# Rotary in two steps, its scratch in the normed input's room, and the filter weights off GpSimd

## The chip, the cores and the metric

The kernel runs on one core of a Trainium2 chip. The metric is the device time of one execution, in microseconds (us). The kernel before took 1338.2 us, the median of 3 runs (1337.94 to 1339.54).

## The reference

A two-layer encoder on 512 tokens of width 1024, all in float32. Only three places matter here:

```
layer 0: mixed = [gated_deltanet, dilated_attention](rmsnorm(x) @ ab_w_in) @ ab_w_out
layer 1: mixed = [retention, hyena](rmsnorm(x) @ cd_w_in) @ cd_w_out
each layer: x = x + mixed;  x = x + conv_ffn(rmsnorm(x))

rope(t):  t1, t2 = halves of each head's 64 columns
          [t1*cos - t2*sin, t1*sin + t2*cos]          # q and k of dilated attention and retention
hyena_filters:  hid = sin(f1*(z @ w1 + b1));  hid = sin(f2*(hid @ w2 + b2))
                filt = (hid @ w3) * exp(-t*deltas)     # a forward and a backward filter
```

## The kernel before

**Tiling.** Activations stand transposed, features on the 128 partitions and the 512 tokens along a row. A float32 product is made of three matmuls of float32r parts (`mm3`, lines 266 to 268): high times high, high times low, low times high. So each weight tile `raw` that a DMA brings is split into `whi` by ScalarE (line 254) and `wlo` by VectorE, or GpSimd when `pool_lo` is set (line 255). `raw` has 3 buffers; `whi` and `wlo` have 4 each, so the cast of a tile waits for the projection four tiles earlier.

**Rotary.** The projections q0, k0, q1, k1 of dilated attention (q0, q1, k0, k1 of retention) leave 128x512 tiles in PSUM (`first0` to `first2`, and `dqk` or `rqk` for the fourth). For each in turn `rope_stack` has ScalarE copy the tile to `rt` (line 455, 2 buffers; from now on "the reading"), four DMAs on SyncE's queue swap halves into `rs` (line 458, 1 buffer), GpSimd multiplies `rs` by the sines (line 459), VectorE multiplies `rt` by the cosines and adds (lines 460, 461), and ScalarE, VectorE and, for the moving operand, GpSimd write the high and low parts (lines 466 to 470). The four PSUM buffers tagged `acc` then take the four accumulators `pt0` to `pt3` of the token-major value projection (`proj_tok`, line 295), whose four weight tiles each hold 6 matmuls for each accumulator: 96 in all.

**Filters.** `hyena_filters` is a generator that `hyena` steps once after each of its twelve column projections (`hap`), apart from the numbers in `HSKIP`, counted from 0. The first step makes the first sine layer (matmul `hm`, line 1098, chain `san` on VectorE, sine `mlp` on ScalarE, line 1078). The second prepares the parts of the last weight `w3` (sum and difference `ws` on GpSimd, `wy` on ScalarE and GpSimd, `wl` on VectorE, zeroed by GpSimd) and makes the second sine layer (matmul `hm`, line 1111, up to `hx`). The third and later ones multiply (`fp`, lines 1131 and 1132) and transform. Between them `turn` transposes the product `u` (line 1209) on TensorE (`tp`, line 1195).

**Order.** Except at the start, a scheduler turns the program into one fixed order for each engine; an instruction that waits holds up all behind it on its engine. The normed input's tiles `xn` (pool `xp`, 2 buffers of 4 KB a partition) are free once TensorE has transposed them.

Of the kernel before, what the change touches and what calls it, by code (L numbers as in the profile page):

```python
# [8 lines left out]
F32 = mybir.dt.float32  # L9
F32R = mybir.dt.float32r  # L10
# [5 lines left out]
S = 512  # L16
# [147 lines left out]
class K:  # L164
# [282 lines left out]
        self.nc.sync.dma_start(rope, self.I["rope"])  # L447
        return rope

    def rope_stack(self, pool, rope, ps, moving, tag, bufs, scale=1.0):  # L450


        nc = self.nc
        t = pool.tile([128, S], F32, tag="rt", name="rt", bufs=2)
        nc.scalar.mul(t, ps, scale)  # L455
        sw = pool.tile([128, S], F32, tag="rs", name="rs", bufs=1)
        for q in range(4):
            nc.sync.dma_start(sw[32 * q:32 * q + 32, :], t[32 * (q ^ 1):32 * (q ^ 1) + 32, :])
        nc.gpsimd.tensor_mul(sw, sw, rope[:, 1, :])
        nc.vector.tensor_mul(t, t, rope[:, 0, :])  # L460
        nc.vector.tensor_add(t, t, sw)
        o = pool.tile([128, 4 if moving else 2, S], F32R, tag=tag, name=tag, bufs=bufs)
        half = [slice(0, 64), slice(64, 128)]
        for e in range(2):
            a, b = half[e], half[1 - e]
            nc.scalar.copy(o[a, e], t[a])
            nc.vector.tensor_sub(o[a, 2 + e] if moving else o[b, e], t[a], o[a, e])
            if moving:
                nc.gpsimd.memset(o[b, 2 + e].bitcast(F32), 0.0)
                nc.gpsimd.tensor_copy(o[b, e], o[a, e])  # L470
        return o

    def mm_stack(self, out, a, b, e, cols):
        self.nc.tensor.matmul(out, a[:, e, cols], b[:, e], start=True, stop=False)
        self.nc.tensor.matmul(out, a[:, e, cols], b[:, 2 + e], start=False, stop=True)
# [14 lines left out]
    def dilated(self, n, tail):  # L490
        nc, I = self.nc, self.I
        V = nc.vector
        with ExitStack() as ctx:
            dp = ctx.enter_context(self.tc.tile_pool(name="dil", bufs=1))
            rope = dp.tile([128, 2, S], F32, name="rope")
            lnc = dp.tile([128, 896], F32, name="lnc")
            v = dp.tile([128, NT, 512], F32, name="dv")
            qk, sm, pT, op = {}, {}, {}, {}
            yh, yl = self.y_tiles()

            def project(p, what, ps=None):
                if ps is None:
                    ps = self.acc(nm="dqk")
                    self.proj_t(self.get(), n, ps)
                qk[p, what] = self.rope_stack(dp, rope, ps, what == "k", "d" + what, 3)

            def scores(p, i):
                st = self.sm.tile([128, 6], F32, tag="st", name="st", bufs=8)
                o = 384 - 128 * i
                for e in range(2):  # L510
                    sp = self.wk(nm="sp")
                    self.mm_stack(sp, qk[p, "q"], qk[p, "k"], e, slice(i * 128, i * 128 + 128))
                    s_ = dp.tile([128, S], F32, tag="smx", name="smx", bufs=6)
                    V.tensor_tensor_reduce(s_, sp, lnc[:, o:o + 512], scale=-0.125, scalar=3e38, op0=ALU.add, op1=ALU.min, accum_out=st[:, e:e + 1])
                    nc.scalar.activation(s_, s_, AF.Exp, scale=-1.0, bias=st[:, e:e + 1], accum_out=st[:, 2 + e:3 + e])
                    sm[p, i, e] = s_
                V.reciprocal(st[:, 4:6], st[:, 2:4])
                for e in range(2):
                    nc.gpsimd.tensor_scalar(sm[p, i, e], sm[p, i, e], st[:, 4 + e:5 + e], 1.0, op0=ALU.mult, op1=ALU.mult)

            def turn(p, i):
                for e in range(2):
                    tp = TPD(self)((128, 4, 128), "tp")
                    for j in range(4):
                        nc.tensor.transpose(tp[:, j, :], sm[p, i, e][:, j * 128:j * 128 + 128], self.ident)
                    t = dp.tile([128, 4, 128], F32, tag="pT", name="pT", bufs=4)
                    (V.tensor_copy if e else nc.scalar.copy)(t, tp)
                    pT[p, i, e] = t

            def pv(p, i):  # L530
                if i == 0:
                    op[p] = self.acc(nm="op")
                for j in range(4):
                    for e in range(2):
                        h = 2 * p + e
                        nc.tensor.matmul(op[p][64 * e:64 * e + 64, i * 128:i * 128 + 128], v[:, j, h * 64:h * 64 + 64], pT[p, i, e][:, j, :], start=(j == 0), stop=(j == 3))
                if i == 3:
                    self.split(yh[p // 2][:, p % 2, :], yl[p // 2][:, p % 2, :], op[p])

            ps = self.first(n, range(4), at=DAT)  # L540
            self.pool_lo = False
            nc.sync.dma_start(rope, I["rope"])
            nc.sync.dma_start(lnc, I["lnc"])
            for i in range(4):
                project(i // 2, "qk"[i % 2], ps[i] if i < 3 else None)
            self.proj_tok(n, lambda t, a: nc.scalar.copy(v[:, t, :], a))
            later = [(2, "q"), (2, "k"), (3, "q"), (3, "k")]
            units = [(p, i) for p in range(4) for i in range(4)]
            for u in range(len(units) + 3):
                if u < len(units):  # L550
                    scores(*units[u])
                if 0 <= u - 2 < len(units):
                    turn(*units[u - 2])
                if 0 <= u - 3:
                    pv(*units[u - 3])
                if later and u in DPROJ[:4]:
                    project(*later.pop(0))
                if u in DPROJ[4:]:
                    next(tail, None)
            return self.by_tile(self.y_list(yh, yl))  # L560
# [430 lines left out]
    def retention(self, n, order):  # L991
        nc, I = self.nc, self.I
        V = nc.vector
        with ExitStack() as ctx:
            rp = ctx.enter_context(self.tc.tile_pool(name="ret", bufs=1))
            rope = self.load_rope(rp)
            gen = rp.tile([128, 4, 896], F32, name="gen")
            ps = self.first(n, order)
            qk = {}
            for i in range(4):  # L1000
                which, s = i // 2, i % 2
                if i < 3:
                    pp = ps[i]
                else:
                    pp = self.acc(nm="rqk")
                    self.proj_t(self.get(), n, pp)
                qk[which, s] = self.rope_stack(rp, rope, pp, which == 0, f"r{which}{s}", 1, 1.0 if which else 0.125)
            v = rp.tile([128, NT, 512], F32, name="rv")
            Z = rp.tile([128, NT, 512], F32, name="rz")
            self.proj_tok(n, lambda t, a: nc.scalar.copy(v[:, t, :], a))  # L1010
# [48 lines left out]
    @staticmethod  # L1059
    def g4(hp, nm, dt=F32):  # L1060
        return hp.tile([128, 2, S], dt, tag="g4", name=nm, bufs=G4)
# [18 lines left out]
    def hyena_filters(self, hp, H):  # L1080


        nc, I = self.nc, self.I
        V = nc.vector
        g4 = lambda nm, dt=F32: self.g4(hp, nm, dt)
# [9 lines left out]
        w3 = g4("w3")[:64]  # L1095
        nc.sync.dma_start(w3, I["hy_w3"][0].rearrange("p (a c) -> p a c", a=2))
        ps = self.wk((64, S), "hm")
# [1 line left out]
        self.sin_layer(hp, h1, ps, bf[:, 0:1], bf[:, 1:2])  # L1099
        self.tables(hp, 0)  # L1100
        yield
        ws = g4("ws")[:64]
        nc.gpsimd.tensor_add(ws[:, 0], w3[:, 0], w3[:, 1])
        nc.gpsimd.tensor_sub(ws[:, 1], w3[:, 0], w3[:, 1])
        wy, wl = g4("wy", F32R), g4("wl", F32R)
        nc.scalar.copy(wy[:64], ws)
        V.tensor_sub(wl[:64], ws, wy[:64])
        nc.gpsimd.memset(wl[64:].bitcast(F32), 0.0)
        nc.gpsimd.tensor_copy(wy[64:], wy[:64])
        ps = self.wk((64, S), "hm")  # L1110
        nc.tensor.matmul(ps, w12[:, 1, :], h1, start=True, stop=True)
        hid = g4("hid")[:64, 0]
# [2 lines left out]
        hx = g4("hx", F32R)[:, 0]  # L1115
        nc.scalar.copy(hx[:64], hid)
        V.tensor_sub(hx[64:], hid, hx[:64])
        dec = []
        for a in range(2):
            dec.append(self.xp.tile([128, 2, S], F32, tag="xn", name=f"dec{a}"))  # L1120
# [4 lines left out]
        for i in range(2):  # L1125
            for par in range(2):
                hs = [g4("hs" + x, F32R) for x in "hl"]
                for t in range(2):
                    c = slice((2 * par + t) * 128, (2 * par + t) * 128 + 128)
                    ps = self.wk(nm="fp")  # L1130
# [11 lines left out]
                for ft in range(2):  # L1142
                    ps = self.wk(nm="hf")
# [30 lines left out]
    def hyena(self, n, yc):  # L1174
# [4 lines left out]
        with ExitStack() as ctx:  # L1179
# [19 lines left out]
            for ct in range(4):  # L1199
                vx = g4("vx")  # L1200
                for which in (2, 1, 0):
# [5 lines left out]
                    if which == 1:  # L1207
                        u = hp.tile([128, 2, 256], F32, tag="u", name="u")
                        V.tensor_mul(u, byp(vx[:, 0]), byp(vx[:, 1]))
                    if 3 * ct + 2 - which not in HSKIP:  # L1210
                        next(filters, None)
# [82 lines left out]
FILLC = 1  # L1294
IA = 3
HT = 6
HSKIP = (2, 3)


def body(k, out):  # L1300
# [55 lines left out]
```

## Time and profile before

| | us |
|---|---|
| median of 3 runs | 1338.2 |
| the profiled execution | 1336.83 |
| its span in the trace | 1335.0 |
| TensorE busy | 1306.7 (98%) |
| VectorE busy | 750.3 (56%) |
| ScalarE busy | 532.3 (40%) |
| GpSimd busy | 152.6 (11%) |

TensorE is busy nearly throughout, so the other engines' totals say little: what counts is where TensorE stood idle, what ended each idle time, and where its granted clock was below full. PE is TensorE, ACT is ScalarE, DVE is VectorE, POOL is GpSimd, SP is SyncE. A row of a timeline has the start, the duration, the engine, the line of the kernel, the operation, output and inputs, and in brackets the idle time just before it with what ended it.

### The profile page before, as it was taken

Reading aid. Unit: us, or ns where it says so; the run is one execution under the profiler, and the core shown is the slowest. Engines: PE = TensorE matmul, PEld = TensorE weight load, DVE = VectorE, ACT = ScalarE, POOL = GpSimd, SP = SyncE. Lnnn points to the kernel's source line nnn. Section 1 sums busy time; section 2 is a strip of 40 time slices with the busy share of each in tenths; the row PEclk is TensorE's granted clock in tenths of the full one; section 3 lists DMA queues with packets and bytes.
Section 4 is the critical chain, followed back from the end, with each engine's and each line's share of the span. In section 5 each row is a group of like instructions: output and inputs, shape, how many; then the busy total and the mean of one; then the engine's idle time right before and its main releaser. Section 6 shows DMA issues by size and latency. Waiting matters only on the chain.

```text
span 1335.0 us, 17713 instructions
## 1 busy us (share of the span) xinstructions
PE 1306.7 (98%) x6977; PEld 1092.9 (82%) x6977; DVE 750.3 (56%) x1105; ACT 532.3 (40%) x892; POOL 152.6 (11%) x180
## 2 busy tenths in 40 slices
PE   7999999899999999999999999999999999999997
PEld 6877888788988888888889786888898888888886
DVE  6677549968654432444436728769754443254432
ACT  4466567233433321233326434442433331133332
POOL 3454120003000000000001202024000000000002
PEclk9999999999999999999999999999999999999999
DMA  7431113411333333333324412320153333233321
GB/s 220 129 90 39 51 32 94 143 50 60 89 116 96 95 95 95 96 99 102 98 79 144 118 48 82 103 87 31 55 152 95 95 95 95 81 115 102 98 79 64
DMA packets 161027, 123.69 MB, mean 93 GB/s; under 512 B 6985, under 2 KB 134477, under 8 KB 160944
## 3 DMA queue, kind: packets, MB, share of 16 engines
q1 hardware_dynamic: 160798, 122.49, 31.1%
q8 instruction: 55, 0.90, 0.3%
q14 instruction: 28, 0.23, 0.1%
q10 hardware_dynamic: 146, 0.07, 0.0%
HBM read 117.30 MB, written 2.10 MB: 89 GB/s over the span
## 4 chain that ended last, share of the span: by engine, by line
PE 83%; DVE 8%; ACT 4%; issue 2%; DMA 1%; POOL 1%; SPq 1%; POOLq 0%; ACTq 0%; DVEq 0%
PE gup L267 11%; PE gup L266 11%; PE gup L268 11%; PE oacc L266 7%; PE oacc L267 7%; PE oacc L268 7%; PE ap L268 1%; PE ap L266 1%; PE ap L267 1%; PE pt L266 1%; PE hap L268 1%; PE hap L267 1%; PE hap L266 1%; PE pt L268 1%; PE pt L267 1%
## 5 line engine op out<-in xcount | busy, mean ns | idle before, releaser
L255 DVE TENSOR_TENSOR wlo<-raw,whi 128x1024 fp32r<-128x1024 f32 x191 | 235.1, 1232 | 317.8 <-ACT whi L254 311.9
L254 ACT CAST whi<-raw 128x1024 fp32r<-128x1024 f32 (+1 forms) x197 | 207.0, 1051 | 430.6 <-PE gup L267 186.1
L266 PE MATMUL gup<-hh,whi 128*128 128x512 f32 x656 | 255.2, 389 | 0.0
L267 PE MATMUL gup<-hl,whi 128*128 128x512 f32 x656 | 255.2, 389 | 0.0
L268 PE MATMUL gup<-hh,wlo 128*128 128x512 f32 x656 | 255.2, 389 | 0.0
L268 PEld LDWEIGHTS gup<-hh,wlo 128*128 128x128 f32 x656 | 123.1, 188 | 25.6
L266 PEld LDWEIGHTS gup<-hh,whi 128*128 128x128 f32 x656 | 123.1, 188 | 25.6
L267 PEld LDWEIGHTS gup<-hl,whi 128*128 128x128 f32 x656 | 123.2, 188 | 25.4
L266 PE MATMUL oacc<-whi,ghi 128*128 128x512 f32 x352 | 137.1, 389 | 0.0
L268 PE MATMUL oacc<-whi,glo 128*128 128x512 f32 x352 | 137.0, 389 | 0.0
L267 PE MATMUL oacc<-wlo,ghi 128*128 128x512 f32 x352 | 136.9, 389 | 0.0
L268 PEld LDWEIGHTS oacc<-whi,glo 128*128 128x128 f32 x352 | 66.1, 188 | 13.7
L266 PEld LDWEIGHTS oacc<-whi,ghi 128*128 128x128 f32 x352 | 66.1, 188 | 13.7
L267 PEld LDWEIGHTS oacc<-wlo,ghi 128*128 128x128 f32 x352 | 66.1, 188 | 13.6
L430 DVE TENSOR_TENSOR sl<-gup,sl 128x512 f32<-128x512 f32 x42 | 29.1, 692 | 81.7 <-PE gup L268 81.7
L315 DVE TENSOR_TENSOR x<-oacc,x 128x512 f32<-128x512 f32 x64 | 43.5, 687 | 51.5 <-PE oacc L268 51.4
L429 ACT ACTIVATE sl<-c 128x512 f32<-128x512 f32 x44 | 27.9, 634 | 89.9 <-DVE c L367 89.9
L266 PE MATMUL first<-hh,whi 128*128 128x256 f32 x192 | 54.9, 288 | 0.0
L267 PE MATMUL first<-hl,whi 128*128 128x256 f32 x192 | 54.4, 284 | 0.2 <-DVE hl L227 0.2
L268 PE MATMUL first<-hh,wlo 128*128 128x256 f32 x192 | 54.2, 283 | 0.0
L266 PE MATMUL pt<-whi,hh 128*128 128x512 f32 x128 | 50.5, 395 | 3.7 <-ACT rt L455 2.5
L105 POOL TENSOR_SCALAR ss<-ss 128x1 f32<-128x1 f32 x16 | 5.0, 313 | 429.6 <-ACT jk L103 429.6
(406 smaller groups left out, 2356.5 us busy)
## 6 DMA issues: line engine op xcount, KB each, us to landing
raw<-in_ffn_w_in_dram SPq DMA_DIRECT2D x88, 512.0 KB, 3.8
raw<-in_ffn_w_out_dram SPq DMA_DIRECT2D x44, 512.0 KB, 3.7
raw<-in_ab_w_in_dram SPq DMA_DIRECT2D x28, 512.0 KB, 3.8
raw<-in_cd_w_in_dram SPq DMA_DIRECT2D x24, 512.0 KB, 4.1
x<-in_x_dram SPq DMA_DIRECT2D x16, 256.0 KB, 5.0
raw<-in_ab_w_out_dram SPq DMA_DIRECT2D x8, 512.0 KB, 3.6
raw<-in_cd_w_out_dram SPq DMA_DIRECT2D x8, 512.0 KB, 3.8
rs<-rt SPq DMA_DIRECT2D x48, 64.0 KB, 2.0
```

Of the source, the lines that this page charges most:

```text
L105: nc.gpsimd.tensor_scalar(ss[:, 1:2], ss[:, 0:1], s, EPS, op0=ALU.add, op1=ALU.add)
L254: self.nc.scalar.copy(hi, raw)
L255: (self.nc.gpsimd if self.pool_lo else self.nc.vector).tensor_tensor(lo, raw, hi, op=ALU.subtract)
L266: mm(out, a[0], b[0], start=start, stop=False)
L267: mm(out, a[0], b[1], start=False, stop=False)
L268: mm(out, a[1], b[0], start=False, stop=stop)
L315: self.nc.vector.tensor_add(xs, acc, xs)
L429: nc.scalar.activation(sl, c, AF.Silu)
L430: nc.vector.tensor_mul(sl, up, sl)
```

## The change

`rope_stack` is cut in two: `rope_in` (reading and the four DMAs) and `rope_out` (everything behind). The second and fourth projection of each group of four take both of their scratch tiles from one `xn` buffer, here called `room`; the first and third keep `rt` and `rs`. The fourth projection's accumulator is taken ahead of the loop. Under `issue_after`, what ScalarE does for the third and fourth rotary parts stands behind the fourth reading. The four projections made later in dilated attention go through both halves as before.

In `hyena_filters` the preparation of `w3` moves behind the second sine layer, with GpSimd's four instructions given to VectorE (sum, difference, zeroing) and ScalarE (copy). `HSKIP` goes from (2, 3) to (1, 3): the second step comes after column 2 and not after column 1.

```diff
-    def rope_stack(self, pool, rope, ps, moving, tag, bufs, scale=1.0):
+    def rope_in(self, pool, ps, scale=1.0, room=None):
         nc = self.nc
-        t = pool.tile([128, S], F32, tag="rt", name="rt", bufs=2)
-        nc.scalar.mul(t, ps, scale)
-        sw = pool.tile([128, S], F32, tag="rs", name="rs", bufs=1)
+        if room is None:
+            t = pool.tile([128, S], F32, tag="rt", name="rt", bufs=2)
+            sw = pool.tile([128, S], F32, tag="rs", name="rs", bufs=1)
+        else:
+            t, sw = room[:, 0], room[:, 1]
+        ins = nc.scalar.mul(t, ps, scale)
         for q in range(4):
             nc.sync.dma_start(sw[32 * q:32 * q + 32, :], t[32 * (q ^ 1):32 * (q ^ 1) + 32, :])
+        return t, sw, ins
+
+    def rope_out(self, pool, rope, t, sw, moving, tag, bufs):
+        nc = self.nc
         nc.gpsimd.tensor_mul(sw, sw, rope[:, 1, :])
...
+    def rope_room(self):
+        return self.xp.tile([128, 2, S], F32, tag="xn", name="room")
...
+            ps.append(self.acc(nm="dqk"))
+            rin = []
             for i in range(4):
-                project(i // 2, "qk"[i % 2], ps[i] if i < 3 else None)
+                if i == 3:
+                    self.proj_t(self.get(), n, ps[3])
+                rin.append(self.rope_in(dp, ps[i], room=self.rope_room() if i % 2 else None))
+                if i < 2:
+                    qk[0, "qk"[i]] = self.rope_out(dp, rope, *rin[i][:2], i == 1, "d" + "qk"[i], 3)
+            with self.tc.issue_after(rin[3][2].ins):
+                for i in (2, 3):
+                    qk[1, "qk"[i % 2]] = self.rope_out(dp, rope, *rin[i][:2], i == 3, "d" + "qk"[i % 2], 3)
...
             for i in range(4):
-                which, s = i // 2, i % 2
...
-                qk[which, s] = self.rope_stack(rp, rope, pp, which == 0, f"r{which}{s}", 1, 1.0 if which else 0.125)
+                if i == 3:
+                    self.proj_t(self.get(), n, ps[3])
+                rin.append(self.rope_in(rp, ps[i], 1.0 if i // 2 else 0.125, self.rope_room() if i % 2 else None))
+                if i < 2:
+                    rot(i)
+            with self.tc.issue_after(rin[3][2].ins):
+                rot(2)
+                rot(3)
...
-        ws = g4("ws")[:64]
-        nc.gpsimd.tensor_add(ws[:, 0], w3[:, 0], w3[:, 1])
-        nc.gpsimd.tensor_sub(ws[:, 1], w3[:, 0], w3[:, 1])
-        wy, wl = g4("wy", F32R), g4("wl", F32R)
-        nc.scalar.copy(wy[:64], ws)
-        V.tensor_sub(wl[:64], ws, wy[:64])
-        nc.gpsimd.memset(wl[64:].bitcast(F32), 0.0)
-        nc.gpsimd.tensor_copy(wy[64:], wy[:64])
         ps = self.wk((64, S), "hm")
...
         V.tensor_sub(hx[64:], hid, hx[:64])
+        ws = g4("ws")[:64]
+        V.tensor_add(ws[:, 0], w3[:, 0], w3[:, 1])
+        V.tensor_sub(ws[:, 1], w3[:, 0], w3[:, 1])
+        wy, wl = g4("wy", F32R), g4("wl", F32R)
+        nc.scalar.copy(wy[:64], ws)
+        V.tensor_sub(wl[:64], ws, wy[:64])
+        V.memset(wl[64:].bitcast(F32), 0.0)
+        nc.scalar.copy(wy[64:], wy[:64])
...
-HSKIP = (2, 3)
+HSKIP = (1, 3)
```

What the scheduler makes of it shows at three places. First ScalarE in retention, around the four readings (lines 455 before, 458 after) and the casts of the rotated parts (`r00`, `r01` are q; `r10`, `r11` are k). Before:

```order
L1019 ACTIVATE gen_6048<-gen_6048 128x896
L466 CAST r00_6238<-rt_6228 64x512 x2
L254 CAST whi_6395<-raw_6393 128x1024
L455 ACTIVATE rt_6266<-first2_6069 128x512
L466 CAST r01_6257<-rt_6247 64x512 x2
L455 ACTIVATE rt_6312<-rqk_6281 128x512
L254 CAST whi_6425<-raw_6423 128x1024
L254 CAST whi_6637<-raw_6635 128x1024
L466 CAST r10_6276<-rt_6266 64x512 x2
```

The same place after:

```order
L458 ACTIVATE rt_6264<-first2_6067 128x512
L1048 ACTIVATE gen_6046<-gen_6046 128x896
L474 CAST r00_6237<-rt_6227 64x512 x2
L254 CAST whi_6391<-raw_6389 128x1024
L474 CAST r01_6255<-room_6246 64x512 x2
L458 ACTIVATE room_6301<-rqk_6226 128x512
L474 CAST r10_6310<-rt_6264 64x512 x2
L254 CAST whi_6421<-raw_6419 128x1024
L474 CAST r11_6318<-room_6301 64x512 x2
```

The third reading has moved ahead of the first casts; the fourth stands behind the casts of `r01` before and after. In dilated attention the fourth reading moves further, from behind the casts of `dk` (second rotary part) to behind those of `dq` (first).

Second TensorE in retention, at the 18th and 19th matmul of the value projection (`pt`). Before:

```order
L266 MATMUL pt2_6331<-whi_6284,hh0_5932 128x512
L267 MATMUL pt2_6331<-wlo_6285,hh0_5932 128x512
L268 MATMUL pt2_6331<-whi_6284,hl0_5934 128x512
L266 MATMUL pt0_6329<-whi_6335,hh0_5932 128x512
L267 MATMUL pt0_6329<-wlo_6336,hh0_5932 128x512
```

After:

```order
L266 MATMUL pt2_6327<-whi_6273,hh0_5930 128x512
L267 MATMUL pt2_6327<-wlo_6274,hh0_5930 128x512
L268 MATMUL pt2_6327<-whi_6273,hl0_5932 128x512
L266 MATMUL pt3_6328<-whi_6273,hh0_5930 128x512
L267 MATMUL pt3_6328<-wlo_6274,hh0_5930 128x512
```

`pt3`, which takes the PSUM buffer that the fourth reading frees, begins after 18 matmuls. Before it begins after 35 in retention and after 36 in dilated attention; there too it is 18 after the change.

Third TensorE in hyena, where the second sine layer's `hm` and the transposes `tp` of `u` stand in the fourth projection (`hap`). Before:

```order
L266 MATMUL hap_7051<-hh0_5932,whi_7010 128x512
L267 MATMUL hap_7051<-hl0_5934,whi_7010 128x512
L1111 MATMUL hm_6985<-mlp_6912,w12_6914 64x512
L1195 MATMUL tp_7032<-ident_76,u_6974 128x128 x4
L268 MATMUL hap_7051<-hh0_5932,wlo_7011 128x512
```

After:

```order
L266 MATMUL hap_7047<-hh0_5930,whi_6975 128x512
L267 MATMUL hap_7047<-hl0_5932,whi_6975 128x512
L1224 MATMUL tp_6997<-ident_76,u_6970 128x128 x4
L1132 MATMUL hm_7015<-mlp_6908,w12_6910 64x512
L268 MATMUL hap_7047<-hh0_5930,wlo_6976 128x512
```

The two change places. Further on, `fp` stands right behind the fifth projection before, and 10 matmuls later, inside the sixth, after. What it waits for on ScalarE stands so after:

```order
L1107 ACTIVATE hid_7017<-san_7019 64x512
L1137 CAST hx_7028<-hid_7017 64x512
L1143 CAST wy_7034<-ws_7031 64x1024
L254 CAST whi_7257<-raw_7255 128x1024
L1146 COPY wy_7034<-wy_7034 64x1024
```

`whi_7257` is the ninth column's weight and takes the buffer of the fifth's. On SyncE's queue the two loads of the decay tables (line 1121, `dec`, in retention) move from ahead of the first rotary DMAs to behind the last, since they take the `xn` buffers that are `room` now, and behind them stand six weight loads.

## Rows read from the trace of the kernel before

**Rows 1.** Page, busy time of each engine over the span

```profile
PE 1306.7 (98%) x6977; PEld 1092.9 (82%) x6977; DVE 750.3 (56%) x1105; ACT 532.3 (40%) x892; POOL 152.6 (11%) x180
```

**Rows 2.** TensorE's waits: who, for whom, us in total, times, longest

```profile
PE pt L266 <- ACT rt L455: 2.5, 2, 1.9
...
PE hm L1111 <- ACT mlp L1078: 2.0, 1, 2.0
```

**Rows 3.** Timeline of TensorE, value projection of dilated attention

```profile
41.48 0.39 PE L266 MATMUL pt<-whi,hh 128*128 128x512 f32 x1
...
50.49 0.50 PE L266 MATMUL pt<-whi,hh 128*128 128x512 f32 x1 [0.69 <-ACT rt L455]
```

**Rows 4.** Timeline of ScalarE there

```profile
40.77 0.62 ACT L466 CAST dq<-rt 64x512 fp32r<-64x512 f32 x1
```

**Rows 5.** Timeline of TensorE, value projection of retention

```profile
736.83 0.39 PE L268 MATMUL rqk<-hh,wlo 128*128 128x512 f32 x1
...
747.24 0.50 PE L266 MATMUL pt<-whi,hh 128*128 128x512 f32 x1 [1.85 <-ACT rt L455]
```

**Rows 6.** Timeline of ScalarE there

```profile
736.83 1.26 ACT L466 CAST r<-rt 64x512 fp32r<-64x512 f32 x2 [1.39 <-DVE rt L461]
...
746.59 0.60 ACT L455 ACTIVATE rt<-rqk 128x512 f32<-128x512 f32 x1 [1.18 <-issue]
```

**Rows 7.** Timeline of VectorE in retention, first rotary part

```profile
734.98 1.21 DVE L255 TENSOR_TENSOR wlo<-raw,whi 128x1024 fp32r<-128x1024 f32 x1
...
736.11 0.68 DVE L461 TENSOR_TENSOR rt<-rt,rs 128x512 f32<-128x512 f32 x1
...
737.48 1.71 DVE L467 TENSOR_TENSOR r<-rt,r 64x512 fp32r<-64x512 f32 x2 [0.69 <-ACT r L466]
```

**Rows 8.** Timeline of GpSimd and VectorE in dilated attention, first rotary part

```profile
36.59 1.82 POOL L459 TENSOR_TENSOR rs<-rs,rope 128x512 f32<-128x512 f32 x1 [11.77 <-DMA rs<-rt]
...
37.41 2.08 DVE L255 TENSOR_TENSOR wlo<-raw,whi 128x1024 fp32r<-128x1024 f32 x1 [0.15 <-ACT whi L254]
```

**Rows 9.** Timeline of TensorE in hyena

```profile
816.81 1.04 PE L1098 MATMUL hm<-mlp,w 33*64 33x512 f32 x2 [0.19 <-DVE vx L367]
...
817.78 0.50 PE L266 MATMUL hap<-hh,whi 128*128 128x512 f32 x1
...
825.63 0.39 PE L267 MATMUL hap<-hl,whi 128*128 128x512 f32 x1
...
828.04 1.66 PE L1111 MATMUL hm<-mlp,w 64*64 64x512 f32 x2 [2.02 <-ACT mlp L1078]
...
832.05 0.40 PE L266 MATMUL hap<-hh,whi 128*128 128x512 f32 x1
...
847.76 0.60 PE L1195 MATMUL tp<-ident,u 128*128 128x128 f32 x4
```

**Rows 10.** Windows: stretch, us, busy by engine, granted clock, DMA share, GB/s

```profile
829.00:830.00 1.00, 1.00 (x3) 0.37 (x3) 0.97 (x3) 0.59 (x1) 0.00 (x0) 0.50 0.00 0
```

**Rows 11.** Timeline of VectorE in hyena, both sine layers

```profile
819.21 1.50 DVE L1070 TENSOR_SCALAR san<-san 64x512 f32<-64x512 f32 x1
...
820.75 1.14 DVE L1071 TENSOR_SCALAR san<-san 64x512 f32<-64x512 f32 x1
...
821.93 1.40 DVE L1076 SCALAR_TENSOR_TENSOR san<-san 64x512 f32<-64x512 f32 x1
...
827.24 0.68 DVE L1209 TENSOR_TENSOR u<-vx 128x512 f32<-128x512 f32 x1
...
831.53 0.41 DVE L1070 TENSOR_SCALAR san<-san 64x512 f32<-64x512 f32 x1
...
833.19 0.67 DVE L1076 SCALAR_TENSOR_TENSOR san<-san 64x512 f32<-64x512 f32 x1
```

**Rows 12.** Timeline of ScalarE in hyena, filter weights

```profile
820.47 1.05 ACT L1106 CAST wy<-ws 64x1024 fp32r<-64x1024 f32 x1 [5.20 <-POOL ws L1104]
```

**Rows 13.** Timeline of VectorE, first us

```profile
0.98 0.17 DVE L587 MEMSET ones<- 128x128 f32 x1
```

More of the change, by code (lines that the diff above doesn't have):

```diff
@@ L504, in project @@
                     self.proj_t(self.get(), n, ps)
-                qk[p, what] = self.rope_stack(dp, rope, ps, what == "k", "d" + what, 3)
+                qk[p, what] = self.rope_out(dp, rope, *self.rope_in(dp, ps)[:2], what == "k", "d" + what, 3)
             def scores(p, i):
@@ L999, in retention, with rot @@
             qk = {}
-            for i in range(4):
-                which, s = i // 2, i % 2
[L1002 to L1006, printed above, removed]
-                qk[which, s] = self.rope_stack(rp, rope, pp, which == 0, f"r{which}{s}", 1, 1.0 if which else 0.125)
+            ps.append(self.acc(nm="rqk"))
+            rin = []
+            def rot(i):
+                which, s = i // 2, i % 2
+                qk[which, s] = self.rope_out(rp, rope, *rin[i][:2], which == 0, f"r{which}{s}", 1)
+            for i in range(4):
+                if i == 3:
[6 more added lines that the diff above has]
+                rot(3)
             v = rp.tile([128, NT, 512], F32, name="rv")
```

## The prediction

> **What bounds the kernel now.** The page first: TensorE is busy 98% of the span [rows 1]; 28.3 us of idle time are all that other engines can give back, apart from a lowered clock. So the second view is TensorE's waits. The reader is to see that two of its lines stand where the change works: `pt` waits for the reading of a rotary projection (line 455), 2.5 us in two places, and `hm` waits 2.0 us for the first sine [rows 2]. Third, the timeline at the three places. In dilated attention the accumulator `pt3` cannot start until the fourth projection's PSUM buffer is read: 0.69 us idle at 50.49 [rows 3]. In retention the same wait is 1.85 us [rows 5]. The bracket of the late reading says "issue" and 1.18 us [rows 6]: what held it is the buffer of `rt`, two for four projections. In hyena `hm` starts at 828.04 after 2.02 us idle [rows 9]. Fourth, the windows there: the granted clock is 0.50 in 829 to 830 [rows 10], that is 1.2 GHz and not 2.4. It fell after that idle time, so the wait costs twice. The rest of the kernel is not touched by the change.
>
> TensorE's pace: between 817.78 and 825.63 lie 34 starts of `hap` (by their places in the order), so (825.63 - 817.78)/34 = 0.23 us for one [rows 9].
>
> **Dilated attention.** After the change no projection waits for `rt`: the second and fourth have the `xn` buffers, which TensorE has done with, the third has the second `rt`. The price is that `pt3` now stands 18 matmuls behind the first and not 36. TensorE comes to it at 41.48 + 18 x 0.23 = 45.6 [rows 3]. On ScalarE the fourth reading stands behind the casts of `dq`, which end at 40.77 + 0.62 = 41.4 [rows 4], and its projection ends at 41.9 (the first `pt` start plus one duration [rows 3]). With 0.60 for itself [rows 6] it is done near 42.5, 3 us early; if the casts slip by 1.3 us (below), 1.7 us early. So the 0.69 us go whole. Bounds: 0 if a later stage gives it back, 0.85 if the slower first matmul (0.50 and not 0.39) goes with it. I take 0.7.
>
> **Retention.** TensorE comes to `pt3` at 737.06 + 18 x 0.23 = 741.2 (the last `rqk` matmul starts at 736.83, one pace earlier [rows 5]). The fourth reading now stands behind the casts of `r01`, and these behind the whole second rotary part. By the rows of before: `r00` is cast 736.83 to 738.09 [rows 6] and its low parts end at 739.2 [rows 7]; the add of the second part, then in VectorE's order, takes 0.68 [rows 7], to 739.9; two casts 1.26, to 741.1; the reading 0.60, to 741.7 [rows 6]. That leaves 0.5 us of wait. But the second part's GpSimd product now comes right after the first's: its four DMAs are issued directly behind the first four, and it falls into the stretch 734.4 to 736 in which VectorE makes `wlo` and the first add. The same meeting is on record in dilated attention: beside the product on GpSimd, `wlo` took 2.08 us [rows 8] and not 1.21 [rows 7], 0.87 us more; with the other VectorE rows of that stretch the add comes up to 1.1 us later. Then the reading ends at 742.8 and the wait is 1.6 us. So the wait that was 1.85 us becomes 0.5 to 1.6, a gain of 0.25 to 1.35; as the row with the meeting is the nearer one I take 0.5. Bound from below: minus 0.5, if GpSimd meets VectorE twice; from above 2.0, if the reading comes in time.
>
> The Trainium skill has a rule for this ("SBUF — State Buffer", Who interferes with whom): a VectorE instruction with two SBUF inputs and a GpSimd one that reads SBUF exclude each other, and the second to start is blocked until the first ends. It speaks against putting the two products together. The trace agrees on the row of 2.08 us; by the rule taken whole the gain here is 0.25 and the sum 4.55 below, without it 1.35 and 5.65.
>
> **Hyena.** From the start at 825.63 to that at 832.05 are 6.42 us [rows 9]. Undisturbed the same work is: `hm` 817.78 - 816.81 = 0.97, four transposes at most 0.60, five `hap` at 0.23 (those at 825.63 and four after the transposes) 1.15; together 2.72 [rows 9]. So the place costs 3.70: the idle 2.02 and 1.68 of half clock and refilling.
>
> Does the wait go? `tp` now stands first and needs `u`, which starts at 827.24 [rows 11]. GpSimd's four instructions leave the stretch. Beside them three steps of the first sine chain took 1.50, 1.14 and 1.40; the second layer's took 0.41 (the row of 831.53, and I take it for line 1071 too) and 0.67 [rows 11]. So the chain is 1.09 + 0.73 + 0.73 = 2.55 shorter. The low part of the filter weight leaves the chain, and a weight split of the same number of elements a lane takes its place. Its cast stands first on ScalarE now, where `wy` stood; it waits for the second projection, which ends near 820.1 (nine starts from 817.78 [rows 9]), and ends 1.05 later [rows 12], at 821.15. The chain would be ready for it at 819.21 + 0.41 + 0.41 + 0.67 = 820.7, so it loses 0.4 there. Then `u` starts at 827.24 - 2.55 + 0.4 = 825.1 and ends 0.68 later, at 825.8. TensorE is at `tp` at 825.63 + 0.23 = 825.86. The sine runs on ScalarE beside `u` and `tp`, so `hm` finds it done. The wait is 0 to 0.2 and the clock has no cause to fall. Gain 3.6; bounds 0 (all comes back at `fp`) and 3.7.
>
> What is late next: `fp`, for VectorE and ScalarE now prepare `w3` behind the second sine layer. On ScalarE the copy of `wy` stands behind the ninth weight's cast, which waits for the end of the fifth projection; cast and copy are 1.05 each if they cost what the cast of `wy` does [rows 12], so `wy` is whole 2.1 us after that end, and TensorE comes to `fp` 10 x 0.23 = 2.3 us after it. 0.2 us to spare. On VectorE sum and difference add 2 x 0.68 and the low part 1.21, by the row of `u` [rows 11] and that of `wlo` [rows 7]. A memset of this size on VectorE is not in the trace: 0.17 us for a 128x128 one [rows 13] makes between 0.17, if it is all start-up, and 8 x 0.17 = 1.4 for 1024 columns; I take 1.2. It changes nothing while the copy of `wy` is later. So I take 0 here, 0 to 0.5.
>
> **Other moves.** On SyncE's queue the loads of the decay tables now wait for the last `room` in retention, near 750, and six weight loads stand behind them; the tables are first used behind `fp`, some 90 us on, and the first of those loads waits for a buffer then anyway. Cost 0; were they late, hyena's first projection would wait for its weight. In dilated attention one weight load stands behind four more DMAs; its tile is the last of four for `pt`. GpSimd loses its filter instructions, which nothing else waits for.
>
> **Sum.** 0.7 + 0.5 + 3.6 = 4.8 us. The profiled execution of 1336.83 would become 1332.0. It is 1.4 under the median of the runs, which I take as the measure: 1338.2 - 4.8 = 1333.4. A difference of 0.2%, 2.7 us, is about what a measurement of this kernel can tell from none.
>
> **Rivals.**
>
> The clock falls all the same. For: `hm` and `tp` are small matmuls, and the fall came within the former of them. Against: `hm` at 816.81 after 0.19 us idle took 0.97 to the next start, as at full clock [rows 9]. Price 1.7: 1335.1.
>
> The wait moves to `fp`. For: only 0.2 us to spare. A wait of 2 us there, as long as that at `hm`, brings the idle time and the clock back, 3.7 us; only the rotary terms stay: 1338.2 - 1.2 = 1337.0, no change that can be told.
>
> Slower: the same wait is long. The place is `wl`, behind memset, `hx` and four weight splits on VectorE. If its chain ends more than 4.8 - 1.7 = 3.1 us after TensorE is there, counting the half clock, the change loses; at 6 us after, 6 + 1.7 - 4.8 = 2.9 lost, 1341.1. Against: by the rows it ends about 0.7 us before TensorE comes.
>
> **How the numbers follow.** Forecast 0.63, clock 0.12, wait at `fp` 0.18, slower 0.07. The likeliest is 1333.4. Its own bounds are 1338.2 - (0.85 + 2.0 + 3.7) = 1331.6 and, with 0 in dilated attention, 0.25 in retention and 0.5 at `fp`, 1338.2 - 3.35 = 1334.9. Run to run another us below; above, the clock's 1335.1 and most of the wait at `fp`. Range 1330.8 to 1336.8. The first two cases are faster by over 0.2%, the third is within, the last slower: 0.75, 0.18, 0.07.
>
> **What would show it.** Right: `pt` no longer waits in dilated attention and waits 0.5 to 1.6 us in retention; neither `hm` nor `tp` waits over 0.3; the granted clock is 1.0 around them; the sine steps of the first layer take 0.41 and 0.67. Wrong: a new line `fp` among TensorE's waits, or a clock of 0.50 near it; `wlo` beside the second GpSimd product in retention not longer than 1.3 us would refute the meeting.

## The result, and the profile after

The changed kernel took 1331.37 us, the median of 5 runs (1330.72 to 1331.76). Five runs of the kernel before on the same chip gave 1337.94 (1335.56 to 1339.54): 0.995 of the time, with a 95% interval of 0.9939 to 0.9961, 6.6 us less. Forecast were 4.8 less, 1333.4. The profiled executions are 6.1 apart (1336.83 and 1330.72; spans 1335.0 and 1328.9).

Where the difference lies, in us from one TensorE start to another, in the two profiled executions:

| from, to | before | after | difference | forecast |
|---|---|---|---|---|
| first matmul to dilated attention's first `pt` | 37.68 | 37.25 | -0.43 | 0 |
| from there to the first score (`sp`) | 22.74 | 21.76 | -0.98 | -0.7 |
| from there through the delta rule, to the first `oacc` behind its first sums (`m32b`) | 211.52 | 211.38 | -0.14 | 0 |
| retention's first `pt` to its first score (`rsp`) | 24.15 | 23.72 | -0.43 | -0.5 |
| from there to the end of the weighted sums (the next `pt`) | 22.00 | 21.55 | -0.45 | 0 |
| hyena's first `hm` to the long convolution's first sum (`ud`) | 80.12 | 76.37 | -3.75 | -3.6 |

All other stages agree within 0.03. TensorE's waits after, the lines that answer to [rows 2] (who, for whom, us in total, times, longest); the line `hm` for the sine is gone, and `fp` is not there:

```profile
PE pt L266 <- ACT room L458: 1.6, 1, 1.6
```

Dilated attention after, timeline of ScalarE and TensorE. The fourth reading ends at 42.69, and the fourth accumulator starts on time at 45.15 (against [rows 3]):

```profile
42.09 0.60 ACT L458 ACTIVATE room<-dqk 128x512 f32<-128x512 f32 x1
...
45.15 0.39 PE L266 MATMUL pt<-whi,hh 128*128 128x512 f32 x1
```

Retention after, timeline of all engines. The fourth projection starts at 730.05. GpSimd's second product starts 0.55 ahead of `wlo`, which takes 2.32 and not the 1.21 of [rows 7]; the first sum follows it at 735.32. The reading comes at 740.73 and TensorE has waited 1.62. At 759.89 VectorE weights the first scores as soon as they are there:

```profile
730.05 0.40 PE L266 MATMUL rqk<-hh,whi 128*128 128x512 f32 x1
...
732.48 0.68 DVE L468 TENSOR_TENSOR rt<-rt,rope 128x512 f32<-128x512 f32 x1
732.53 1.79 POOL L467 TENSOR_TENSOR room<-room,rope 128x512 f32<-128x512 f32 x1 [0.92 <-DMA room<-room]
...
733.08 2.32 DVE L255 TENSOR_TENSOR wlo<-raw,whi 128x1024 fp32r<-128x1024 f32 x1
...
735.32 0.68 DVE L469 TENSOR_TENSOR rt<-rt,rs 128x512 f32<-128x512 f32 x1
...
740.73 0.60 ACT L458 ACTIVATE room<-rqk 128x512 f32<-128x512 f32 x1
...
741.38 0.50 PE L266 MATMUL pt<-whi,hh 128*128 128x512 f32 x1 [1.62 <-ACT room L458]
...
759.89 4.87 DVE L1058 TENSOR_TENSOR sd<-rsp,gen 128x512 f32<-128x512 f32 x8 [3.54 <-PE rsp L487]
```

The Trainium skill ("SBUF — State Buffer", Who interferes with whom) has the second of the two blocked until the first ends: GpSimd's product ends at 734.32, 1.21 more makes 735.53. The trace agrees within 0.13: `wlo` ended at 735.40.

Hyena after, timeline of all engines (against [rows 9, 11, 12]). The first layer's steps take 0.41 and 0.68, `u` starts at 822.62, and `tp` and `hm` stand right behind the projection's matmuls. The memset took 0.91. The copy of `wy` ends at 837.66, and TensorE is at `fp` at 837.82:

```profile
816.83 0.41 DVE L1099 TENSOR_SCALAR san<-san 64x512 f32<-64x512 f32 x1
...
817.73 0.68 DVE L1105 SCALAR_TENSOR_TENSOR san<-san 64x512 f32<-64x512 f32 x1
...
822.62 0.68 DVE L1238 TENSOR_TENSOR u<-vx 128x512 f32<-128x512 f32 x1
...
823.47 0.60 PE L1224 MATMUL tp<-ident,u 128*128 128x128 f32 x4
...
823.99 1.07 PE L1132 MATMUL hm<-mlp,w 64*64 64x512 f32 x2
...
834.97 0.91 DVE L1145 MEMSET wl<- 64x1024 f32 x1 [0.16 <-issue]
...
836.61 1.05 ACT L1146 CAST wy<-wy 64x1024 fp32r<-64x1024 f32 x1
...
837.82 0.39 PE L1160 MATMUL fp<-wy,hx 128*128 128x512 f32 x1
```

The window that answers to [rows 10], same columns, has the clock at 1.00:

```profile
823.00:825.00 2.00, 2.00 (x10) 0.86 (x8) 1.20 (x3) 2.00 (x4) 0.00 (x0) 1.00 0.00 1
```

### The profile page after: what moved, and what is told of

It is laid out like the page before. It is cut to its first block, busy times and chain, and to the rows that moved or that the text cites. A ratio compares the mean times of both kernels' runs of the same rounds, so it can differ in the third digit from the quotient of the medians.

```text
span 1328.9 us, 17694 instructions
## 1 busy us (share of the span) xinstructions
PE 1304.8 (98%) x6977; PEld 1093.1 (82%) x6977; DVE 755.1 (57%) x1108; ACT 532.7 (40%) x893; POOL 147.9 (11%) x176
## 4 chain that ended last, share of the span: by engine, by line
PE 87%; DVE 7%; ACT 3%; issue 1%; POOL 0%; DMA 0%; SPq 0%; POOLq 0%; ACTq 0%; DVEq 0%
PE gup L267 11%; PE gup L268 11%; PE gup L266 11%; PE oacc L266 7%; PE oacc L267 7%; PE oacc L268 7%; PE first L267 2%; PE first L266 2%; PE first L268 2%; PE pt L266 2%; PE pt L268 2%; PE pt L267 2%; PE hap L267 1%; PE hap L266 1%; PE hap L268 1%
```

## The experiments

Medians and ranges in us; each ratio is against runs of the kernel before on the same chip. Where a kernel keeps the old rotary, its text calls `rope_in` and `rope_out` one right behind the other.

| kernel | median (range; runs) | ratio, 95% interval |
|---|---|---|
| dilated attention's edit alone | 1334.87 (1333.51 to 1336.75; 10) | 0.998, 0.997 to 0.9989 |
| retention's edit alone | 1335.03 (1334.30 to 1338.69; 11) | 0.9982, 0.9971 to 0.9993 |
| hyena's edits alone | 1333.50 (1332.67 to 1335.82; 7) | 0.9969, 0.9958 to 0.9979 |
| weights later, table as before | 1333.62 (1332.81 to 1333.98; 6) | 0.9973, 0.9961 to 0.9985 |
| skip table alone | 1338.71 (1335.13 to 1341.23; 10) | 1.0014, 1.0003 to 1.0025 |
| changed, second product on VectorE | 1331.50 (1331.17 to 1331.97; 4) | 0.9955, 0.994 to 0.9969 |
| changed, parts early but off GpSimd | 1332.64 (1331.17 to 1333.38; 6) | 0.9969, 0.9958 to 0.9981 |
| changed, parts late but on GpSimd | 1332.83 (1332.40 to 1333.39; 6) | 0.9972, 0.9961 to 0.9983 |
| changed, once more | 1330.87 (1330.31 to 1332.67; 5) | 0.9961, 0.9948 to 0.9973 |
| changed, fourth reading first | 1329.61 (1328.98 to 1329.80; 5) | 0.9933, 0.9921 to 0.9946 |
| the same, once more | 1329.13 (1328.96 to 1329.62; 5) | 0.9946, 0.9933 to 0.9958 |
| the kernel before, once more | 1337.78 (1334.99 to 1339.02; 10) | 1.0006, 0.9996 to 1.0015 |

### Dilated attention alone

The kernel before with the edit in `dilated` only: retention keeps `rope_in` and `rope_out` one behind the other, hyena is that of before.

```diff
+                rin.append(self.rope_in(dp, ps[i], room=self.rope_room() if i % 2 else None))
+            with self.tc.issue_after(rin[3][2].ins):
```

> The kernel before with the rotary edit in dilated attention alone. Distances are from one TensorE start to another in the profiled execution, first matmul of the value projection to first score: 22.74 us before, 21.76 with the whole change. Theory (the forecast's first term, enlarged by what the trace after shows): the two waits for the fourth reading and the slow matmuls behind them go whole, 22.74 becomes 21.8, 0.9 to 1.0 us, and nothing else in the kernel moves: 0.95 us less than before. Rival (the first stage's 0.43 us between the kernel's first matmul and the first of the value projection, 37.68 before and 37.25 after, comes from this edit too, by tiles that lie elsewhere): 37.25 here as well, 1.4 us less in all.

Measured: 21.76, and 37.59 ahead of it, so the first stage's 0.43 is not the edit's. In the 14 profiled executions of all kernels that stage took 37.25 in the profile after and 37.58 to 38.35 in the others. The median fell by 3.3 and not by 0.95; why, these runs do not settle (the spread of the kernel before, below, bears on it). Medians cannot size the parts here: against the same 22 runs of the kernel before the three edits alone give 3.3, 3.15 and 4.7 us, 11.1 in all, where the whole change gave 6.6 in its own comparison; and the kernel before has medians of 1338.18 and 1336.77 in two sets of runs on the chip of these three. So the parts are sized by stages.

Retention here is that of before, and shows what the scores' 0.45 was. In the timeline of TensorE and VectorE the last rotary part stands on VectorE until 761.3, and the weighting of the scores waits behind it (22.41 for that stage, against 21.55):

```profile
759.87 1.40 DVE L475 TENSOR_TENSOR r<-rt,r 64x512 fp32r<-64x512 f32 x2 [0.69 <-ACT r L474]
761.30 4.87 DVE L1050 TENSOR_TENSOR sd<-rsp,gen 128x512 f32<-128x512 f32 x8
...
762.14 0.47 PE L486 MATMUL rsp<-r,r 128*128 128x512 f32 x1 [0.41 <-DVE sd L1050]
```

### Retention alone

```diff
+                rin.append(self.rope_in(rp, ps[i], 1.0 if i // 2 else 0.125, self.rope_room() if i % 2 else None))
+            with self.tc.issue_after(rin[3][2].ins):
```

> The kernel before with the rotary edit in retention alone. First matmul of the value projection to first score: 24.15 us before, 23.72 with the whole change; first score to the end of the weighted sums: 22.00 and 21.55. Theory: the reading's wait stays near 1.6 us, the stage gives 0.43, and the scores give 0.45 more, because the last rotary part no longer stands on VectorE when the first score is to be weighted; 0.9 us less than before in all. Rival (the forecast's term alone): 0.5 us, and the 0.45 of the scores belongs to something else, so that 22.00 stays.

The scores took 21.55: the 0.45 is this edit's, and the rival falls. All eight profiles with the edit have 21.54 or 21.55 there, the six without it 21.92 to 22.56. But the first stage of the two took 25.62. Behind the wait the clock fell to 0.50 (timeline of TensorE, then a window with the columns of [rows 10]):

```profile
743.84 0.50 PE L266 MATMUL pt<-whi,hh 128*128 128x512 f32 x1 [1.95 <-ACT room L458]
```

```profile
746.00:748.00 2.00, 2.00 (x6) 1.60 (x5) 1.42 (x2) 0.44 (x1) 0.39 (x2) 0.50 0.60 91
```

This profiled execution took 1338.28, among the longest of eleven; seven took 1334.3 to 1335.4.

### Hyena alone, and its two edits apart

> The kernel before with both edits in hyena alone (filter weights later and off GpSimd, and the skip table). First hyena filter matmul to first of the long convolution's sums: 80.12 us before, 76.37 with the whole change. Theory: 3.75 us here too, independent of the rotary edits, the three parts add up to the whole: 0.95 + 0.9 + 3.75 = 5.6 us of the 6.2 between the profiled executions, and the rest (0.43 in the first stage, 0.14 in the delta rule) is scatter between executions. Rival: hyena's gain needs the decay tables' loads that the rotary edit moved, or the first stage's 0.43 is tied to it: another number than 3.75 here, or 37.25 in the first stage.

Measured: 76.40, with 37.59 in the first stage; the theory holds for hyena, and its rival falls. That the three parts add up to the whole is not shown, since the profile of retention's edit alone had the lower clock. The two edits apart, the weights first (against both together):

```diff
-HSKIP = (1, 3)
+HSKIP = (2, 3)
```

> The kernel before with the filter weight parts later and off GpSimd, the skip table as before: the filter matmul of the second layer stands ahead of the transposes again. First hyena filter matmul to first of the long convolution's sums: 80.12 us before, 76.37 with both edits. Theory: the sine chain without GpSimd beside it is the whole gain. In the changed kernel the sine ends at 823.36 and TensorE would come to the filter matmul at 823.24: it waits 0.1 to 0.2 us, the clock stays, 76.4 to 76.6. Rival: the skip table is needed for it: the matmul still waits 0.5 us or more, the clock falls behind it, 78 to 80.

76.64, 0.04 above the theory's range: of 3.75 us, 3.48 come without the skip table. Timeline: the first step takes 0.41 again, and `hm` starts at 826.28, one pace and 0.09 behind the `hap` at 825.96:

```profile
819.55 0.41 DVE L1082 TENSOR_SCALAR san<-san 64x512 f32<-64x512 f32 x1
...
825.96 0.39 PE L267 MATMUL hap<-hl,whi 128*128 128x512 f32 x1
826.28 1.07 PE L1115 MATMUL hm<-mlp,w 64*64 64x512 f32 x2
```

The skip table alone is the kernel before with `HSKIP = (1, 3)`:

> The kernel before with the skip table alone: the transposes ahead of the filter matmul, the filter weight parts on GpSimd beside the first sine layer as before. Theory: the transposes need the product of the two gates, which ends at 827.92 in the kernel before, and TensorE is there at 825.86: it waits 2 us for it, the clock falls as before, and hm1-to-sums stays at 80.1 (80.12 before; 76.37 with both edits): no gain, within 0.3 us of before. Rival: the order of the two is what matters, 78 or less.

The wait is there, at `tp`, and the runs show no gain (0.14% more). In the profiled execution, the shortest of the ten, the clock stayed, and so the stage took 78.76 and not 80.1; that is not the rival's 78, since the wait is whole. The theory's falling clock did not come in this execution. Whether the transposes behind the wait, in place of `hm`, had a part in that is not shown; the median speaks against a steady gain of 1.4 us from it:

```profile
827.80 0.66 PE L1207 MATMUL tp<-ident,u 128*128 128x128 f32 x4 [2.01 <-DVE u L1221]
```

```profile
828.00:830.00 2.00, 2.00 (x9) 0.93 (x8) 2.00 (x3) 1.68 (x3) 0.00 (x0) 1.00 0.01 3
```

### Off GpSimd, or later

The changed kernel with the eight lines of the preparation moved back ahead of the second `hm`, on VectorE and ScalarE:

> The changed kernel with the filter weight parts back in their old place (beside the first sine layer), but on VectorE and ScalarE. First hyena filter matmul to first of the long convolution's sums: 80.12 us before, 76.37 in the changed kernel. Theory (what counts is how much VectorE has to do ahead of the sine, the gate product and the weight splits): sum and difference add 0.68 each to the chain, the gate product ends near 823.0 and not 823.3 less the split that is put off, and the put-off split of the weight ends near 830 where its projection starts near 828.5: a wait of 1 to 2 us there, 78 to 80. Rival (GpSimd's company alone made the old place bad): the sine steps take 0.41 and 0.68, nothing waits over 0.3 us, 76.4 to 77.2.

The theory fell: 76.97, and apart from a wait of 0.64 that `tp` has near the end of this stage in all profiles, neither `tp` nor `hm` nor a later projection waits over 0.3. The steps in the timeline of VectorE:

```profile
818.80 0.41 DVE L1099 TENSOR_SCALAR san<-san 64x512 f32<-64x512 f32 x1
...
820.67 0.68 DVE L1105 SCALAR_TENSOR_TENSOR san<-san 64x512 f32<-64x512 f32 x1
```

The other half, late in the program but on GpSimd:

```diff
-        V.tensor_add(ws[:, 0], w3[:, 0], w3[:, 1])
+        nc.gpsimd.tensor_add(ws[:, 0], w3[:, 0], w3[:, 1])
```

(and so for difference, memset and copy)

> The changed kernel with the filter weight parts in their new place in the program, but sum, difference, memset and copy on GpSimd again. First hyena filter matmul to first of the long convolution's sums: 80.12 us before, 76.37 in the changed kernel. Theory (GpSimd has nothing else to do there and starts them as soon as the weight has landed, near 815 to 817, whatever stands ahead of them on the other engines): they stand beside the first sine layer again, the steps take 1.50 and 1.14 again, the gate product comes 1.8 us later, TensorE waits 1.5 us or more ahead of the transposes, 78 to 80. Rival (they start behind the second sine layer, as their place says): sine steps 0.41 and 0.68, 76.4, or a wait at the filter product for the copy, 77 to 78.

77.92, between the two. GpSimd did start at once, beside the first layer, as the theory has it. But only one step met it, since the memset now came after 6.19 us of idle time that ended with the sine (`mlp`); so `tp` waits 0.53 and not 1.5, and `fp` 0.39 for the copy:

```profile
815.96 1.27 POOL L1140 TENSOR_TENSOR ws<-w 64x512 f32<-64x512 f32 x1 [10.88 <-DMA w<-in_hy_w_dram]
...
817.85 1.51 DVE L1099 TENSOR_SCALAR san<-san 64x512 f32<-64x512 f32 x1
...
825.18 0.65 PE L1224 MATMUL tp<-ident,u 128*128 128x128 f32 x4 [0.53 <-DVE u L1238]
825.27 0.95 POOL L1145 MEMSET wl<- 64x1024 f32 x1 [6.19 <-ACT mlp L1107]
...
839.02 0.50 PE L1160 MATMUL fp<-wy,hx 128*128 128x512 f32 x1 [0.39 <-POOL wy L1146]
```

So what hyena gains is for the most part that GpSimd leaves: of 3.75 us the other engines without the later place give 3.15, the later place without the other engines 2.2. Both have the new skip table. The two overlap and do not add: in the one profile of each the clock stayed at 1.00 there, and that alone is about 1.4 of the 3.75 (80.12 against the 78.76 of the skip table alone).

### The meeting in retention

```diff
-        nc.gpsimd.tensor_mul(sw, sw, rope[:, 1, :])
+        (nc.vector if dve else nc.gpsimd).tensor_mul(sw, sw, rope[:, 1, :])
```

with `dve` for retention's second part, and the fourth reading held behind the casts by `issue_after`.

> The changed kernel; in retention the second rotary part's product with the sine table is on VectorE, ahead of its sum, and no longer on GpSimd beside the weight split; the order of the casts and the reading on ScalarE is the changed kernel's. First matmul of the value projection to first score: 24.15 us in the kernel before, 23.72 in the changed one, with a wait of 1.62. Theory (the meeting with GpSimd stretches the split from 1.21 to 2.32 us and the rest follows): the split takes 1.2, the first part's sum starts 1.0 earlier, VectorE gets 0.7 more behind it, and the reading ends 0.6 earlier: wait 1.0, stage 23.1. Rival (the split is long for another reason): it stays at 2.3, the 0.7 comes on top, wait 2.3, stage 24.4.

The split took 1.21, so the meeting is what stretched it; in the seven other profiles with retention's edit, where the product stays on GpSimd, it took 2.31 or 2.32. But the stage took 24.28. Timeline: ScalarE's first decay step waited 1.05 for the small load `ld`, which it did not in the profile after, and all of ScalarE and VectorE came 1 us later:

```profile
721.42 2.91 ACT L1047 ACTIVATE gen<-rel,ld 128x896 f32<-128x896 f32 x3 [1.05 <-DMA ld<-in_ret_log_decay_dram]
...
735.02 1.21 DVE L255 TENSOR_TENSOR wlo<-raw,whi 128x1024 fp32r<-128x1024 f32 x1
...
742.95 0.50 PE L266 MATMUL pt<-whi,hh 128*128 128x512 f32 x1 [2.20 <-ACT room L458]
```

How far VectorE's first rotary product stands behind the fourth projection's start (after: 732.48 - 730.05 = 2.43) therefore sets the wait. That distance follows `ld`: in 13 of the 14 profiles it is 2.32 to 2.34 us plus ScalarE's wait for `ld`, and in the profile after, which shows no such wait, 2.43. In the five profiled executions of kernels with the changed retention it was 2.43, 2.57, 2.71, 2.76 and 2.86, and the wait 1.62, 1.76, 1.88, 1.95 and 2.05: 0.81 to 0.83 less each time. Here it was 3.39; 2.58 would be due by that line, drawn on beyond its last point, and 2.20 came. So the gain from taking GpSimd out is about 0.4, not the 0.6 expected, and the rival's 0.7 of loss is out.

### The reading first, a version that beats both

```diff
-                if i < 2:
+                if i < 1:
                     rot(i)
             with self.tc.issue_after(rin[3][2].ins):
+                rot(1)
                 rot(2)
```

> The changed kernel with one more step in retention: the fourth reading on ScalarE ahead of the casts of the second rotary part, and behind it as before. ScalarE is idle for 1.07 us ahead of those casts (it waits for VectorE's sum at 739.41), and the fourth projection has ended by 735.7. Theory: the reading then runs in that idle time, from 738.4 to 739.0, TensorE comes to its buffer at 739.6, so the wait of 1.62 us goes whole and the rotary parts behind are no later (they end at 752.6, the first score stands at 757.5): 1.7 us less than the changed kernel, 1329.7. Rival: the wait only moves, to the first scores (the rotary parts become the last to come, or the weighting on VectorE starts late as it did in the kernel before): 0 to 0.5 us less.

1329.61, and 21.76 from the first `pt` to the first score; the scores keep 21.55. The reading stands in ScalarE's idle time and ends at 739.63; TensorE comes at 739.98 and does not wait (timeline):

```profile
739.04 0.59 ACT L458 ACTIVATE room<-rqk 128x512 f32<-128x512 f32 x1
...
739.98 0.39 PE L266 MATMUL pt<-whi,hh 128*128 128x512 f32 x1
```

Beside the changed kernel once more:

> The changed kernel once more, beside the next one on the same chip: 1331.4 us within 0.5. Its own wait in retention follows the landing of the decay row, which ScalarE's first decay steps wait for: with VectorE's first rotary product 2.43 us behind the first matmul of the fourth projection the wait was 1.62; each tenth later adds a tenth. Where that wait reaches 2 us the clock may fall behind it, and the run is then 1.5 to 2 us longer.

> The changed kernel with the fourth reading in retention ahead of the casts of the second rotary part, once more, beside the changed kernel: 1329.6 us within 0.5, 1.7 less than the changed kernel. Theory: it does not depend on when the decay row lands, since the reading has 1 us to spare. Rival: with a late decay row a wait comes back and the difference shrinks under 1 us.

1330.87 and 1329.13: 1.7 us apart, as the theory has it. With ScalarE's wait for `ld` at 0.49 in the first profile and 0.19 in the second, the fourth accumulator waits in neither. The ten runs of this version (up to 1329.80) all lie under the ten of the changed kernel (from 1330.31). The changed kernel's own wait was 2.05, and the clock stayed at 1.00 behind it.

### The kernel before, once more

> The kernel before once more, with another profiled execution. The runs of the kernel before spread from 1335.4 to 1340.6 us at mean clocks from 0.997 down to 0.993, those of the changed one from 1330.7 to 1331.8 at 0.997. The profile of retention's edit alone has the clock at 0.50 behind the wait of 1.9 us there, the first profile of the kernel before has not. Theory (that place falls in some executions and not in others, and each fall costs 1.5 to 2 us): an execution of 1337.5 us or more shows a stretch at 0.50 in retention, first matmul of the value projection to first score 25.6 to 26.1 in place of 24.15; one of 1336.3 or less shows 23.5 to 24.2 there. Rival (the spread comes from the first stage's loads): the stage keeps 24.1 whatever the time, and the 37.6 us before the value projection of dilated attention vary in its place.

Not told apart: the profiled execution took 1337.06, between the two ranges named. Its clock fell in the delta rule and in hyena, as in the first profile, and not in retention (24.73 there, with `ld` 0.87 late). The first stage took 37.58 (37.68 in the first profile), which speaks against the rival without settling it. What an execution of 1339 us looks like was not seen.

## Why the prediction was right, and where it was not

**Sign and mechanism** were right: the rotary wait goes in dilated attention and stays in retention, the sine chain loses GpSimd, and `tp`, `hm` and `fp` find their inputs. The rivals with a falling clock or a wait at `fp` did not come.

**Hyena, 3.6 forecast, 3.75 measured.** The steps came nearly to the tenth. The first `hm` starts 2.38 earlier than before (814.43, not 816.81); the forecast's 825.1 for `u` is then 822.72 (came: 822.62), and its 825.86 for `tp` is 823.48 (came: 823.47). The copy of `wy` was to be ready 0.2 ahead of TensorE and was 0.16 ahead: near enough that the rival with a wait at `fp` was no idle one. The memset, taken at 1.2, took 0.91.

**Dilated attention, 0.7 forecast, 0.98 measured; above the bound of 0.85.** The mechanism was right and the size was not. The forecast took the bracket, 0.69. A bracket counts from the modelled end of the matmul before, 0.39 behind its start, while the next would have started 0.23 behind it. In the timeline of the kernel before:

```profile
49.41 0.39 PE L268 MATMUL pt<-whi,hl 128*128 128x512 f32 x1
...
50.83 0.40 PE L267 MATMUL pt<-wlo,hh 128*128 128x512 f32 x1
```

With the start at 50.49 between them [rows 3]: 1.08 + 0.34 where two paces make 0.46, so 0.96 lost. That is the term that was too small.

**Retention, 0.5 forecast, 0.88 measured, and in another place.** The meeting took `wlo` to 2.32, and the wait was 1.62, the upper end named. The step that failed is the one that priced this place by the wait at `pt3` alone. Its fall from before to after, 0.43, is for the most part the landing of `ld`: the product stood 2.78 behind in the kernel before and 2.43 after. Timeline of the kernel before:

```profile
721.37 2.92 ACT L1017 ACTIVATE gen<-rel,ld 128x896 f32<-128x896 f32 x3 [0.45 <-DMA ld<-in_ret_log_decay_dram]
...
731.59 0.40 PE L266 MATMUL rqk<-hh,whi 128*128 128x512 f32 x1
...
734.37 0.68 DVE L460 TENSOR_TENSOR rt<-rt,rope 128x512 f32<-128x512 f32 x1
```

In the execution of dilated attention's edit alone, with retention as before, it stood 2.32 behind, and the stage took 23.47, less than the 23.72 after. At nearly the same landing, 2.56 with hyena's edits alone and 2.57 with the parts late but on GpSimd, the stage took 23.85 with the old retention and 23.81 with the new. So at equal landing this stage gains next to nothing. What the edit gives is in the scores (22.41 there, 21.55 after): the last rotary part no longer stands on VectorE ahead of their weighting. The forecast had not followed the rotary parts past the value projection.

**What no term covered**: 0.43 in the first stage and 0.14 in the delta rule. Both vary as much between executions of other kernels: the delta rule's stage took 211.30 to 211.72 in the 14 profiles, and the first stage was the shortest of all in the profile after. So they are luck of that execution. 4.8 + 0.28 + 0.38 + 0.15 + 0.57 makes the 6.2 of the table. The half us more between the medians lies within the spread of the kernel before.

The median of 1331.37 is below 1331.6, the best that the forecast's own terms allowed; what holds it in the range is the us added for scatter. So the hit owes something to luck as well as to the mechanism.

## What to carry to other kernels

Size a wait on TensorE from start to start against the undisturbed pace, not by the idle time in the bracket. Where a step is moved, follow what it frees beyond the next wait: here the scores behind, not the reading, repaid retention's edit. And when an accumulator's buffer is what is waited for, put its reading ahead of work that nobody waits for yet: one line more gave 1.7 us.

## What the runs showed of the hardware

A wait of the same length is followed by a lower clock in one execution and not in the next. In retention waits of 1.88 and 1.95 us were followed by 0.50 and cost 1.6 us more (25.57 and 25.62, where 24.0 and 24.05 were due if each us of wait adds a us to the stage); waits of 2.05 and 2.20 were not. Windows of the kernel with early parts (wait 1.88) and of the changed kernel once more (2.05), which have the same code in retention; the granted clock is the third number from the end:

```profile
744.00:746.00 2.00, 2.00 (x6) 1.52 (x6) 1.58 (x2) 0.28 (x1) 0.40 (x2) 0.50 0.53 88
```

```profile
744.00:746.00 2.00, 2.00 (x10) 1.65 (x10) 1.90 (x2) 0.00 (x0) 0.91 (x1) 1.00 0.42 100
```

In hyena the same 2.0 us at `hm` were followed by it in all four profiles that have that wait (both of the kernel before, and those of dilated attention's and of retention's edit alone), and 2.01 us at `tp` were not in that of the skip table alone, 1.4 us apart. There the order differs too, so that hyena does not part the order from the execution; retention does.

Not every fall costs time. In the delta rule the clock stood at 0.50 in 270 to 272 in the kernel before, and that stage took 211.52; with dilated attention's edit alone it stayed at 1.00 from 264 to 276, and the stage took 211.72.

The kernel before has waits of about 2 us in two of the places changed here, and 22 of its runs spread over 5.2 us at mean clocks from 0.993 to 0.997; the version with the fourth reading first, which has neither, spread over 0.8 in ten. Of the 22, the seven at 0.997 took 1335.38 to 1336.91 and the twelve at 0.995 or less 1338.05 to 1340.62, so the long runs are those with the lower clock. In which places it fell in them is not shown, as no execution of 1339 us was profiled; the longest that was, retention's edit alone with 1338.28, had it at 0.50 in the delta rule, in retention and behind `hm`.
